# Moving weight-sum transfers, half of a compression and the score matmuls in a decoder-block kernel

## Chip, cores and metric

The kernel runs on one core of one Trainium2 chip. The metric is the device time of one execution in microseconds (us), from runs on the chip, taken as the median of several executions. Beside it there is a hardware profile of one execution, with a record for every instruction of the engines: PE (TensorE, matmuls), PEld (its weight loads), DVE (VectorE), ACT (ScalarE), POOL (GpSimd) and SP (SyncE, which here only issues transfers).

## The reference

One layer of a decoder over 256 positions with 2048 channels, batch 1, float32 throughout:

```
h = rms_norm(x);  p = h @ w_in            # columns: A 2048 | B 2048 | q 1024 | kv 1536 | 48 gates | merge 6144
A: a*sigmoid(g) -> causal depthwise conv (31 taps) -> layer_norm -> silu -> @ w_a_out
B: gelu(uv); u * (tril(W_s) @ layer_norm(v) + b) per chunk of 128, 8 groups -> @ w_b_out
C: 16 heads of 64 in 4 kv groups, three attentions with the same q, summed under sigmoid gates:
     compressed: kc, vc = silu(blocks of 32, stride 16, @ w1) @ w2;  softmax(q kc) vc
     selected:   softmax over 4 blocks of 64 (all 4 are chosen, as top_n = min(16, 4))
     window:     softmax over the last 512 positions (here: all earlier ones)
   -> @ w_c_out
y = (gA*A + gB*B + gC*C) @ w_o;   x = x + rms_norm(y)
u = causal_dwconv3(rms_norm(x) @ w_up)    # 2 x 5632 columns
x = x + rms_norm((silu(u_g) * u_v) @ w_down)
```

## The kernel before

**Number format and main stream.** Every large product is made from operands split into a high part in fp32r (`hi`) and a remainder (`lo`): hi·hi, hi·lo and lo·hi are added up in PSUM. Weights come from HBM in pieces of 128x1024 float32 (512 KB) by `fetch` (L114, issued by SP into five `wraw` buffers in turn). ACT makes `whi` from each (L199), DVE makes `wlo` (L200), and PE multiplies. A piece that feeds the token-major products (`mm_t`, L248 to L251) lasts for twelve matmuls of 512 columns. In order, PE works through: the value half of branch B; the projection columns of A, of u, of the compressed k and v (`wf_c`, first four), of the other k (`wf_c`, last four, tile `kkv`), of v and the head gates, and of q (`wf_q`, tile `qf`); then `branch` (L1148), in which for each of four column blocks `cb` the merge gates of B (`pg`, 96 matmuls) and B's output product (`py<-..Bt`, 48 matmuls) are made; `outs_a` (L1208), A's output product (`py<-..At`, four times 48); the four passes `gates_7` (L1301) for the other merge gates, with C's output product; `w_o`; the feed-forward's up projection (44 rounds, from about 860 us to 1340 us); and `w_down`.

**Seven-product form and the sums of weights.** `gates_7`, `w_o` and `w_down` make some pairs of k-tiles by a form with seven block products in place of eight (class `Seven`, L1041). It needs sums of weight blocks, and these are made by DMA: `ahead_steps` (L134) lists, for 16 + 4 + 33 quads of blocks, copies from HBM to a DRAM tile `ahead` and transfers that add onto it (three to five steps a quad, 204 steps in all). `ahead_by(mark, n)` (L157) puts on POOL's queue a tiny copy `tick<-mark`, which waits until `mark` has been computed, and then the next `n` steps of the list. `pooled` (L124) keeps all of these in one order. The list is thus fixed, and each call only sets when its next part may go out. What is left when the up projection begins is spread over its 44 rounds. The first quads are read back by SP in the first `gates_7` pass (`qa<-ahead`), the last in `w_down`.

**Side work.** Work that belongs to no product of the main stream is written as generators in a queue `bg`. `pump(ns)` (L100) is called after each piece of the main stream and emits steps of `bg` until their stated costs reach `ns` (6500 in `branch` and `outs_a`); `until(name)` emits until a mark is set. Towards the attention the queue holds `cmp_prep(0)` and `cmp_prep(1)` (L681: sums of k or v with the position table, on POOL's memset, DVE and ACT), `cmp_gen(0)` and `cmp_gen(1)` (L701: four 512 KB pieces of `w1` each, 32 matmuls `zp` with 256 columns, then `zs` on ACT, `hp` on PE, tanh, and `kcp` for k or `vcp` for v), and `attn()` (L978). `hold("outputs")` stops the queue until `branch` has come to its block 1. `attn` first runs several generators in turn (`in_turn`, L967, one step of each): `lnz_gen` (L595, the normalised and activated output of A's convolution, tile `At`), `cmp_attn(1)` (L808, the compressed attention of the second 128 positions, ending in `pct`), and the scores of the first attention unit. Then it sets mark `A`, for which `outs_a` waits, and goes through eight units (position half, pair of kv groups, selected or window) with `scores`, `weights` and `values`. The last of them is complete, at the latest, where the first `gates_7` pass calls `attended` (L1315).

**Scores.** q and k are plain float32 and a head has 64 dimensions, so one score matmul uses 64 rows of PE. Two heads lie in the two halves of the partitions (`half`), and `in_turns` (L846) chains their matmuls (r = 1, then 0, for one or two heads of the group at a time, or four) so that they follow each other. Each float32 score matmul shows as two matmul records. The same helper chains the products of probabilities and values (`O`). The PSUM for all side work is a pool of four banks (`bank`, L88).

**What sets the order.** The program is written in Python order, but the order of instructions on each engine is decided by the framework's planner, which simulates the engines and takes the ready instruction of the highest priority; an instruction emitted earlier has the higher priority. `tc.issue_after(ins)` forces an order, and `tc.high_priority(offset=PR)` (PR = 1000) lets an instruction count as if it had been emitted that much earlier. On the chip each engine then works through its own list strictly in order.

Of the kernel before, what the change touches and what calls it, by code (L numbers as in the profile page):

```python
# [64 lines left out]
def block(ctx: ExitStack, tc: tile.TileContext, x, xf, x0, fp, cst, rows, sgw, w1, w2, wf_a, wt_bv, wf_bu, wf_c,  # L65
# [688 lines left out]
        while name not in marks:  # L754
            yield debt[0]

    for kv in range(2):
        bg.append(cmp_prep(kv))
        if kv == 0:
            bg.append(hold("outputs"))  # L760
        bg.append(cmp_gen(kv))

    kkv = s8([128, 2, 1024], F32, "kkv")
    kk = kkv[:, 0].rearrange("p (g b t) -> p g b t", g=2, b=2)
    for i in range(4):
        pc = ftile(wf_c[4 + i], hT)
        fsum(pc, kk[:, i % 2, i // 2], rb=rb)
        ahead_by(kk[:, i % 2, i // 2, 0:1], 1)
        pump(BUDGET)
    vsw = kkv[:, 1].rearrange("p (t c) -> p t c", t=2)  # L770
    gsg = P1.tile([128, 2, 48], F32, name="gsg")
# [22 lines left out]
    for i in range(8):  # L794
        pq = ftile(wf_q[i], hT)
        fsum(pq, qf[:, i], scale=0.125, rb=rb)
        ahead_by(qf[:, i, 0:1], 2 + i % 2)
        pump(BUDGET)


# [2 lines left out]
    def apart(work):  # L803

        for ns in work:
            yield 2.0 * ns
# [39 lines left out]
    def in_turns(work):  # L846


        last = None
        for out, lhsT, rhs, start, stop in work:  # L850
            with ExitStack() as order:
                if last is not None:
                    order.enter_context(tc.issue_after(last))
                last = PE.matmul(out, lhsT=lhsT, rhs=rhs, start=start, stop=stop, skip_group_check=True).ins  # L854

    half = [slice(0, 64), slice(64, 128)]

    class Unit:
# [8 lines left out]
        def scores(self):  # L867
            qt, gg, br = self.at
            nk = (qt + 1) * 128
            mk = cs[:, K_MK + 256 - nk:K_MK + 256]  # L870
            hpb = 512 // nk
            ep = s8([128, 2, 4, 256], F32, f"ep{self.nm}")
            e = self.e = [ep[:, r] for r in range(2)]
            m = self.m = P1.tile([128, 2, 8], F32, tag="am", bufs=2, name="am" + self.nm)
            for b in range(4 // hpb):
                ps = [bank([128, hpb, nk], f"s{self.nm}{b}{r}") for r in range(2)]
                in_turns([(ps[r][:, jj], qf[half[r], gg * 4 + b * hpb + jj, qt * 128:qt * 128 + 128],
                           kk[half[r], gg, br, 0:nk], True, True) for jj in range(hpb) for r in (1, 0)])
                for jj in range(hpb):
                    j = b * hpb + jj  # L880
                    for r in range(2):
                        V.tensor_tensor_reduce(e[r][:, j, 0:nk], ps[r][:, jj], mk, 1.0, -3e38, ALU.add, ALU.max,
                                               m[:, r, j:j + 1])
                        yield nk * 1.05 + 130
            V.tensor_scalar(m[:, :, 0:4], m[:, :, 0:4], -1.0, None, op0=ALU.mult)
# [92 lines left out]
    def attn():  # L978

        units = [Unit(qt, gg, br) for qt in (1, 0) for gg in range(2) for br in range(2)]  # L980
        yield from in_turn(lnz_gen(), apart(cmp_attn(1)), apart(units[0].scores()))
        marks.add("A")
        Ct_box["t"] = s16(P1, [128, 8, 2, T], R, "Ct")
        for n, u in enumerate(units):
            if n + 1 < len(units):
                if n == 1:
                    yield from in_turn(apart(cmp_attn(0)), units[n + 1].scores())
                else:
                    yield from units[n + 1].scores()
            if u.at[2] == 0:  # L990
                V.tensor_mul(spread, pct[u.at[0]][:, u.at[1]][:, None, :].to_broadcast([128, 4, 128]),
                             cs[:, K_RJ:K_RJ + 4][:, :, None].to_broadcast([128, 4, 128]))
            yield from u.weights()
            if SUMS_AT <= n < SUMS_AT + 4:
                yield from input_sums(n - SUMS_AT)
            if u.at[2] == 0:
                O = bank([128, 4, 128], "O" + u.nm)
            yield from u.values(O)
# [149 lines left out]
    def branch():  # L1148

        for cb in range(4):  # L1150
            pg = [PS.tile([128, 512], F32, tag="acc", name=f"pg0{cb}{t}") for t in range(2)]
            for q in range(4):
                hs = granule(wt_g[cb * 4 + q])
                for k in range(4 * q, 4 * q + 4):
                    hi, lo = hs[(k % 4) // 2]
                    c = slice((k % 2) * 512, (k % 2) * 512 + 512)
                    for t in range(2):
                        ts = slice(t * 128, t * 128 + 128)
                        with ExitStack() as order:
                            if (cb, k) == (1, 0):  # L1160
                                order.enter_context(tc.issue_after(norm["v"]))
                            mm_t(pg[t], hT[:, k, 0, ts], hT[:, k, 1, ts], hi[:, c], lo[:, c], k == 0, k == KT - 1)
                if (cb, q) == (0, 2):
                    until("m")
                    debt[0] = 0.0
                elif q < 3:
                    if (cb, q) == (1, 2):
                        marks.add("outputs")
                    pump(BUDGET)
            tgs = {}  # L1170
            for t in range(2):
                for a in range(2):
                    tgs[t, a] = q1(f"mg0{cb}{t}{a}")
                    with tc.high_priority(offset=int(PR)):
                        gated[0] = S.activation(tgs[t, a], pg[t][:, a * 256:a * 256 + 256], AF.Tanh,
                                                scale=rh[:, t:t + 1]).ins
            marks.add("gates")
            pump(BUDGET)
            py = [PS.tile([128, 512], F32, tag="acc", name=f"py0{cb}{t}") for t in range(2)]
            for q in range(2):  # L1180
                hs = granule(wt_p[cb * 2 + q])
                if cb == 0 and q == 0:
                    until("B")
                act = Bt_box["t"]
                for k in range(4 * q, 4 * q + 4):
                    hi, lo = hs[(k % 4) // 2]
                    c = slice((k % 2) * 512, (k % 2) * 512 + 512)
                    for t in range(2):
                        ts = slice(t * 128, t * 128 + 128)
                        with ExitStack() as order:  # L1190
                            if (cb, k) == (0, 7):
                                until("v")
                                debt[0] = max(debt[0], 0.0)
                                order.enter_context(tc.issue_after(norm["v"]))
                            pe_last[0] = mm_t(py[t], act[:, k, 0, ts], act[:, k, 1, ts], hi[:, c], lo[:, c], k == 0, k == 7)
                if q == 0:
                    pump(BUDGET)
            for t in range(2):
                for a in range(2):
                    cc = slice(cb * 512 + a * 256, cb * 512 + a * 256 + 256)  # L1200
                    y = mac[:, t, cc]
                    with tc.high_priority(offset=int(PR)):
                        V.scalar_tensor_tensor(y, tgs[t, a], 1.0, py[t][:, a * 256:a * 256 + 256], op0=ALU.add,
                                               op1=ALU.mult)
            ahead_by(mac[:, 0, cb * 512:cb * 512 + 1], (8, 8, 8, 8)[cb])
            pump(BUDGET)

    def outs_a():  # L1208

        for cb in range(4):  # L1210
            py = [PS.tile([128, 512], F32, tag="acc", name=f"py1{cb}{t}") for t in range(2)]
            for q in range(2):
                hs = granule(wt_p[(4 + cb) * 2 + q])
                if cb == 0 and q == 0:
                    until("A")
                for k in range(4 * q, 4 * q + 4):
                    hi, lo = hs[(k % 4) // 2]
                    c = slice((k % 2) * 512, (k % 2) * 512 + 512)
                    for t in range(2):
                        ts = slice(t * 128, t * 128 + 128)  # L1220
                        pe_last[0] = mm_t(py[t], At[:, k, 0, ts], At[:, k, 1, ts], hi[:, c], lo[:, c], k == 0, k == 7)
                if q == 0:
                    pump(BUDGET)
            for t in range(2):
                with tc.high_priority(offset=int(PR)):
                    V.tensor_copy(ya[:, t, cb * 512:cb * 512 + 512], py[t])
            if cb < 2:
                ahead_by(ya[:, 0, cb * 512:cb * 512 + 1], (8, 4)[cb])
            pump(BUDGET)

    def m_sums(n):
# [772 lines left out]
```

## Time and profile before

| | |
|---|---|
| median of 3 runs | 1563.44 us (1559.46 to 1569.31) |
| time of the profiled execution | 1563.63 us |
| its span, first to last instruction | 1561.9 us |
| busy: PE, DVE, ACT, POOL | 1551.4, 1322.3, 970.2, 220.9 us |
| mean granted TensorE clock | 0.998 |
| HBM read, written | 416.45 MB, 90.44 MB |

All times in the profile are in us from the start of the span, unless marked ns. Consecutive matmuls overlap, and the profile shows for each a duration that includes its way through the array (390 ns for 512 columns). The distance from one start to the next is what a matmul costs in a stream; it is read from the start times in the timeline (16 matmuls of 512 columns in 3.65 us). Where PE waits for less than that overlap, it counts as busy.

### The profile page before, as it was taken

The numbers are of one execution on the slowest core, as the hardware profiler recorded it, in microseconds if no ns is written. First come the engines' busy times: TensorE is split into PE (matmuls) and PEld (weight loads), VectorE is DVE, ScalarE is ACT, GpSimd is POOL, SyncE is SP. The second block draws the span as 40 slices with busy tenths as digits, with TensorE's granted clock in tenths as the row PEclk, the third lists the DMA queues.
The fourth block names the chain that finished last, engine by engine and source line by source line (L and its number), as shares of the span: only waits on it lengthen the run. The fifth ranks groups of instructions, "written<-read, shape, count | busy, mean of one in ns | idle before, by whom it ended". The sixth has DMA issues, their size and how long they took to land.

```text
span 1561.9 us, 23350 instructions
## 1 busy us (share of the span) xinstructions
PE 1551.4 (99%) x8101; PEld 1315.6 (84%) x8101; DVE 1322.3 (85%) x2233; ACT 970.2 (62%) x1536; POOL 220.9 (14%) x349
## 2 busy tenths in 40 slices
PE   9999999999999999999999999999999999999998
PEld 8888889887777778888888888888888888888887
DVE  7899999876766579978886898888888887899898
ACT  7644454455677776656665766566666666577774
POOL 1011351221102100000000032222222221100000
PEclk9999999999999999999999999999999999999999
DMA  9687998999779867777774699999999999989896
GB/s 369 195 268 234 273 300 246 296 303 288 236 215 256 223 230 262 247 227 259 268 256 164 205 301 309 306 335 290 287 280 283 282 284 281 316 287 346 313 375 218
DMA packets 130711, 426.13 MB, mean 273 GB/s; under 512 B 15008, under 2 KB 16784, under 8 KB 129824
## 3 DMA queue, kind: packets, MB, share of 16 engines
q1 hardware_dynamic: 99648, 329.46, 60.2%
q0 software_dynamic: 30368, 94.52, 25.7%
q8 instruction: 63, 1.03, 0.3%
q10 hardware_dynamic: 576, 0.66, 0.1%
q14 instruction: 56, 0.46, 0.1%
HBM read 416.45 MB, written 90.44 MB: 325 GB/s over the span
## 4 chain that ended last, share of the span: by engine, by line
PE 97%; DMA 1%; DVE 1%; ACT 1%; issue 0%; DVEq 0%; ACTq 0%
PE ps L228 29%; PE ps L235 15%; PE pg L1056 8%; PE pd1a L1056 4%; PE pd0b L1056 4%; PE pd0a L1056 3%; PE pd1b L1056 3%; PE py L250 3%; PE py L251 3%; PE py L249 3%; PE poa L1056 2%; PE pg L251 1%; PE pg L250 1%; PE pg L249 1%; PE s L854 1%; PE po L249 1%
## 5 line engine op out<-in xcount | busy, mean ns | idle before, releaser
L200 DVE TENSOR_TENSOR wlo<-wraw,whi 128x1024 fp32r<-128x1024 f32 (+1 forms) x344 | 418.2, 1221 | 92.3 <-ACT whi L199 73.3
L199 ACT ACTIVATE whi<-wraw 128x1024 fp32r<-128x1024 f32 (+1 forms) x344 | 361.8, 1057 | 212.0 <-PE ps L228 117.8
L228 PE MATMUL ps<-h2T,whi 128*128 128x512 f32 x1360 | 317.2, 390 | 0.0
L228 PEld LDWEIGHTS ps<-h2T,whi 128*128 128x128 f32 x1360 | 252.4, 188 | 50.4
L235 PEld LDWEIGHTS ps<-h2T,wlo 128*128 128x128 f32 x1360 | 169.4, 192 | 3.6
L235 PE MATMUL ps<-h2T,wlo 128*128 128x256 f32 x1360 | 170.7, 283 | 0.0
L228 PE MATMUL ps<-hT,whi 128*128 128x512 f32 x640 | 151.9, 390 | 0.0
L228 PEld LDWEIGHTS ps<-hT,whi 128*128 128x128 f32 x640 | 117.9, 188 | 23.0
L1012 DVE TENSOR_TENSOR wlowraw<-wraw,whiwraw 128x1024 fp32r<-128x1024 f32 x74 | 89.7, 1222 | 26.6 <-ACT whiwraw L1012 24.6
L556 DVE SCALAR_TENSOR_TENSOR cv<-hb,fps,cv 128x256 f32<-128x256 f32 x240 | 105.9, 491 | 0.1
L1012 ACT ACTIVATE whiwraw<-wraw 128x1024 fp32r<-128x1024 f32 x74 | 77.9, 1059 | 40.4 <-PE py L251 11.8
L1615 ACT ACTIVATE fa<-fs,fps 128x256 f32<-128x256 f32 x88 | 52.8, 600 | 54.1 <-DVE fs L274 52.3
L235 PEld LDWEIGHTS ps<-hT,wlo 128*128 128x128 f32 x640 | 81.1, 191 | 2.5
L235 PE MATMUL ps<-hT,wlo 128*128 128x256 f32 x640 | 82.8, 283 | 0.0
L1056 PE MATMUL pg<-whiwraw,hT 128*128 128x512 f32 x256 | 82.3, 395 | 0.0
L129 POOL DMA_DIRECT2D ahead<-in_wt_dq_dram x91 | 68.1, 901 | 87.1 <-DMA ahead<-in_wt_dq_dram 87.1
L129 POOL DMA_DIRECT2D ahead<-ahead x53 | 43.5, 822 | 245.4 <-DMA ahead<-in_wt_dq_dram 103.8
L271 ACT ACTIVATE t<-ps 128x256 f32<-128x256 f32 x125 | 47.5, 382 | 49.0 <-PE ps L235 26.3
L129 POOL COPY tick<-gh 128x1 f32<-128x1 f32 x44 | 37.5, 853 | 186.3 <-ACT gh L1623 186.3
L1056 PEld LDWEIGHTS pg<-whiwraw,hT 128*128 128x128 f32 x256 | 47.9, 188 | 10.4 <-issue 0.2
L1616 DVE SCALAR_TENSOR_TENSOR fa<-fs,fps,fa 128x255 f32<-128x255 f32 x88 | 42.4, 481 | 16.6 <-ACT fa L1615 16.5
L272 DVE TENSOR_TENSOR t<-ps,t 128x256 f32<-128x256 f32 x125 | 52.4, 420 | 0.5 <-ACT t L271 0.5
(2520 smaller groups left out, 3317.9 us busy)
## 6 DMA issues: line engine op xcount, KB each, us to landing
wraw<-in_wf_up_dram SPq DMA_DIRECT2D x176, 512.0 KB, 6.6
ahead<-in_wt_dq_dram POOLq DMA_DIRECT2D x74, 512.0 KB, 9.8
wraw<-in_wt_p_dram SPq DMA_DIRECT2D x48, 512.0 KB, 6.4
wraw<-in_wt_dq_dram SPq DMA_DIRECT2D x33, 512.0 KB, 6.0
wraw<-in_wf_a_dram SPq DMA_DIRECT2D x32, 512.0 KB, 5.1
ahead<-in_wt_gq_dram POOLq DMA_DIRECT2D x32, 512.0 KB, 9.9
wraw<-in_wt_g_dram SPq DMA_DIRECT2D x32, 512.0 KB, 7.1
wraw<-in_wt_gp_dram SPq DMA_DIRECT2D x32, 512.0 KB, 4.9
```

The costliest lines, as they stand in the source:

```text
L129: in_pool[:] = [op(*args, **kw).ins]
L199: S.activation(hi[:, :n], raw[:, :n], AF.Copy)
L200: V.tensor_sub(lo[:, :n], raw[:, :n], hi[:, :n].bitcast(F32))
L228: ins = PE.matmul(ps, lhsT=ws[k // 8][0][:, c:c + 128], rhs=mov[:, k], start=bool(k == 0 and first), stop=bool(k == n - 1 and not first), ...
L235: ins = PE.matmul(ps[:, 1], lhsT=ws[k // 8][1][:, c:c + 128], rhs=mov[:, k, 0], start=bool(k == 0 and not first), stop=bool(k == n - 1 and ...
L249: PE.matmul(ps, lhsT=xh, rhs=hi, start=first, stop=False)
L250: PE.matmul(ps, lhsT=xh, rhs=lo, start=False, stop=False)
L251: return PE.matmul(ps, lhsT=xl, rhs=hi, start=False, stop=last).ins
L556: V.scalar_tensor_tensor(ca[:, j], hb[:, j, k:k + T], w(j, k), ca[:, j], op0=ALU.mult, op1=ALU.add)
L1012: seq[eng] = [op(*args, **kw).ins]
L1056: ins = PE.matmul(bank, lhsT=a[x], rhs=w[y], start=first and j == 0, stop=bool(last and j == 2), skip_group_check=more).ins
L1615: S.activation(a, s, AF.Identity, bias=fps[:, C_FB + f:C_FB + f + 1], scale=w[2])
```

## The change

Three things are edited.

1. *Weight-sum transfers.* `ahead_by` is taken out of the four `kkv` tiles (4 steps, and 4 ticks). For q it issues 2 steps a tile where it was 2 and 3 by turns (4 steps fewer). In `branch`, block 0 issues 4 where it was 8 (4 fewer). In `outs_a`, block 1 issues 8 where it was 4, and block 2 issues 4 where there was no call (8 more, one more tick). The remaining 4 come in the up projection, among the rest that is spread there.
2. *Side work.* `cmp_gen(1)`, the second half of the compression, leaves its place in `bg` behind `cmp_prep(1)` and becomes one of the three generators that `attn` runs in turn, with `lnz_gen` and the first unit's scores. `cmp_attn(1)` leaves that group and runs by itself after it, ahead of mark `A`. There its steps count their stated cost once where `apart` made them count twice.
3. *Score runs.* In `in_turns`, every matmul but the first of a chain gets the high priority. In `Unit.scores` the two PSUM banks are requested for r = 1 first and then for r = 0.

```diff
-    for kv in range(2):
-        bg.append(cmp_prep(kv))
-        if kv == 0:
-            bg.append(hold("outputs"))
-        bg.append(cmp_gen(kv))
+    bg.append(cmp_prep(0))
+    bg.append(hold("outputs"))
+    bg.append(cmp_gen(0))
+    bg.append(cmp_prep(1))
...
         fsum(pc, kk[:, i % 2, i // 2], rb=rb)
-        ahead_by(kk[:, i % 2, i // 2, 0:1], 1)
         pump(BUDGET)
...
         fsum(pq, qf[:, i], scale=0.125, rb=rb)
-        ahead_by(qf[:, i, 0:1], 2 + i % 2)
+        ahead_by(qf[:, i, 0:1], 2)
         pump(BUDGET)
...
                 if last is not None:
                     order.enter_context(tc.issue_after(last))
+                    order.enter_context(tc.high_priority(offset=int(PR)))
...
-                ps = [bank([128, hpb, nk], f"s{self.nm}{b}{r}") for r in range(2)]
+                ps = [bank([128, hpb, nk], f"s{self.nm}{b}{r}") for r in (1, 0)][::-1]
...
-        yield from in_turn(lnz_gen(), apart(cmp_attn(1)), apart(units[0].scores()))
+        yield from in_turn(cmp_gen(1), lnz_gen(), apart(units[0].scores()))
+        yield from cmp_attn(1)
         marks.add("A")
...
-            ahead_by(mac[:, 0, cb * 512:cb * 512 + 1], (8, 8, 8, 8)[cb])
+            ahead_by(mac[:, 0, cb * 512:cb * 512 + 1], (4, 8, 8, 8)[cb])
...
-            if cb < 2:
-                ahead_by(ya[:, 0, cb * 512:cb * 512 + 1], (8, 4)[cb])
+            if cb < 3:
+                ahead_by(ya[:, 0, cb * 512:cb * 512 + 1], (8, 8, 4)[cb])
```

## The prediction

> **What bounds the kernel.** I read the page first, for who is busy and what the chain that ended last is made of.
>
> ```profile
> span 1561.9 us, 23350 instructions
> ...
> PE 1551.4 (99%) x8101; PEld 1315.6 (84%) x8101; DVE 1322.3 (85%) x2233; ACT 970.2 (62%) x1536; POOL 220.9 (14%) x349
> ...
> q0 software_dynamic: 30368, 94.52, 25.7%
> ...
> PE 97%; DMA 1%; DVE 1%; ACT 1%; issue 0%; DVEq 0%; ACTq 0%
> ```
>
> PE is the bound: 99% busy and 97% of the chain. No product is removed by the change, so only two things can shorten it: time in which PE waits or runs at a lower clock, and pairs of matmuls that could run at once and don't. The second hides in "busy", so I look for it in start times. The first I look for by stage, with the view that gives busy times for stretches (columns: PE, PEld, DVE, ACT and POOL busy, granted clock, DMA share, GB/s).
>
> ```profile
> 335.00:360.00 25.00, 24.88 (x122) 20.75 (x120) 20.17 (x32) 12.53 (x16) 6.09 (x16) 1.00 1.02 307
> 360.00:380.00 20.00, 17.69 (x94) 14.53 (x95) 14.67 (x23) 15.29 (x23) 2.10 (x5) 1.00 0.87 312
> 380.00:400.00 20.00, 18.65 (x82) 15.19 (x82) 11.18 (x15) 8.40 (x12) 3.63 (x6) 0.91 0.99 296
> 430.00:500.00 70.00, 70.00 (x344) 53.76 (x343) 48.72 (x120) 50.45 (x118) 9.95 (x17) 1.00 0.83 232
> 500.00:548.00 48.00, 48.00 (x258) 33.63 (x256) 26.06 (x96) 37.68 (x110) 7.29 (x11) 1.00 0.85 229
> 548.00:570.00 22.00, 20.89 (x94) 14.48 (x93) 11.59 (x18) 16.23 (x39) 0.00 (x0) 1.00 0.65 209
> 880.00:1340.00 460.00, 460.00 (x2645) 407.16 (x2644) 396.08 (x693) 286.53 (x458) 104.26 (x154) 1.00 0.95 287
> 395.47:398.88 3.41, 3.41 (x9) 2.63 (x8) 3.27 (x8) 3.14 (x5) 0.06 (x1) 0.50 1.09 320
> ```
>
> PE is idle for 0.12 + 2.31 + 1.35 = 3.8 us between 335 and 400, with the DMA engines full (shares of 1.02, 0.87 and 0.99), and for 1.1 us between 548 and 570. Behind the last of the first group 3.41 us pass at a clock of 0.50, worth 1.7 us. In the up projection (880 to 1340) nothing is lost, though the DMA share is 0.95. Who released these waits, from the view of waits between 340 and 400, and then the chain of that stretch (start, length):
>
> ```profile
> PE hp L720 <- ACT zs L716: 1.3, 1, 1.3
> PE py L249 <- ACT whi L199: 1.3, 2, 0.7
> PE py L250 <- DVE wlo L200: 0.6, 1, 0.6
> PE pg L250 <- DVE wlo L200: 0.5, 1, 0.5
> ```
>
> ```profile
> 352.94 9.74 DMA wraw<-in_wt_p_dram
> ...
> 380.87 11.16 DMA wraw<-in_wt_g_dram
> ...
> 393.19 0.28 ACT zs L716
> 393.51 1.16 PE hp L720 x8
> ```
>
> All four have one cause. Weight pieces land late, ACT's `whi` is held, and what stands behind it in ACT's order (`zs` at 393.19) or depends on it (`wlo`) is late for PE. Two transfers make the chain here, of 9.7 and 11.2 us. How late that is, from the page's and this stretch's (335 to 400) DMA issues, median us to landing last:
>
> ```profile
> wraw<-in_wt_p_dram SPq DMA_DIRECT2D x48, 512.0 KB, 6.4
> wraw<-in_wt_p_dram SPq DMA_DIRECT2D x8, 512.0 KB, 10.9
> ```
>
> So 3.7 us of waits and 1.7 us of half clock, 5.4 us, is what this stage can give back.
>
> **Part 1, the transfers.** Their number and their engine time, from the view of line 129:
>
> ```profile
> L129 POOL DMA_DIRECT2D ahead<-in_wt_dq_dram x91: 544/830/2217, 442.4 to 1331.7; - x91
> L129 POOL DMA_DIRECT2D ahead<-ahead x53: 801/814/874, 92.6 to 1341.5; - x53
> L129 POOL DMA_DIRECT2D ahead<-in_wt_gq_dram x48: 533/816/897, 72.9 to 352.4; - x48
> L129 POOL DMA_DIRECT2D ahead<-in_wt_oq_dram x12: 627/822/1133, 352.9 to 441.8; - x12
> ```
>
> These are 204 steps, and the software queue that carries them took 25.7% of 1561.9 us = 401 us of all sixteen engines: 2.0 us a step at most, some of it being other transfers. Four steps fewer at block 0 take 8 us out of the 25 us from 335 on, a share of 0.70 where 1.02 is. The eight taken from `kkv` and q would have gone out before, where PE loses nothing; they let POOL, which works strictly in order, reach block 0's and 1's calls, and the memsets of the compression that stand behind them, without arrears. POOL also loses four ticks and gains one, at no cost: nothing on the path waits for POOL but these transfers and memsets.
>
> Where do they go? Eight go behind `outs_a`'s blocks 1 and 2, from about 500 us on: 16 us of DMA. Free there are 0.15 x 48 + 0.35 x 22 = 14.9 us by the rows above. That is just enough, if they spread. If they don't, the first seven-form pass, which fetches on SP in the same stretch, meets what 335 to 400 met: at worst the same 5.4 us. At best it costs nothing, as from 880 to 1340, where a share of 0.95 costs PE nothing. I take 1.0, near the lower end, because the share at 430 to 548 leaves room and PE has no wait there now. Four steps in the up projection add 8 us to 460, a share of 0.97: nothing, and if that cover failed, the pieces there would land later for a few rounds. No sum becomes late: the steps for the gate passes are out by block 2 of `branch` (64 steps in the list's order), and the last pass that reads them comes after `outs_a`, three passes on.
>
> **Part 2, the moved half.** `cmp_gen(1)` issues four fetches of `w1` and one of `w2` on SP, four `whi` and `wlo`, two `zs`, 32 matmuls `zp`, then `hp` and `vcp`. All of this remains, at the same price on PE; it only moves, in turn with `lnz_gen` and the scores, so its four pieces, 2 MB beside the main stream, come spread out. The main stream's fetches no longer stand behind four extra ones in the five buffers. `lnz_gen` comes forward and is needed only by `outs_a`; a block of `branch` lies between. `cmp_attn(1)` starts later; `O` of the first unit waits for its `pct`, and behind that `O` on PE's order stands the main stream. The first two kinds of wait in the list (1.3 + 0.6 + 0.5 = 2.4 us, for `whi` and `wlo`) I count as gone, since both the transfers and the pieces that crowd them leave. The wait for `zs` with the half clock (1.3 + 1.7 = 3.0 us) goes from here, but the same `hp` behind the same `zs` behind a `whi` comes again somewhere after 400: I count half, 1.5 us, between 0 and 3.0. Together 3.9 us.
>
> The row of the clock says that it fell within 2 us of a wait of 1.3 us. [...]
>
> **Part 3, the runs of scores.** From the timeline of PE (start, length; the next row's start is the end of the run): a cut run and a whole one with 256 columns, then a whole and a cut one with 128.
>
> ```profile
> 404.81 0.70 PE L854 MATMUL s<-kkv,qf 64*128 64x256 f32 x2
> 405.43 0.50 PE L251 MATMUL pg<-whi,hT 128*128 128x512 f32 x1
> ...
> 407.47 1.13 PE L854 MATMUL s<-kkv,qf 64*128 64x256 f32 x6
> 408.52 0.50 PE L250 MATMUL pg<-wlo,hT 128*128 128x512 f32 x1
> ...
> 452.40 1.13 PE L854 MATMUL s<-kkv,qf 64*128 64x256 f32 x8
> 453.46 0.50 PE L250 MATMUL pg<-wlo,hT 128*128 128x512 f32 x1
> ...
> 531.61 1.16 PE L854 MATMUL s<-kkv,qf 64*128 64x128 f32 x16
> 532.71 0.50 PE L250 MATMUL py<-wlo,At 128*128 128x512 f32 x1
> ...
> 542.42 0.49 PE L854 MATMUL s<-kkv,qf 64*128 64x128 f32 x2
> 542.83 0.50 PE L1056 MATMUL pg<-whiwraw,hT 128*128 128x512 f32 x1
> ...
> 544.43 1.16 PE L854 MATMUL s<-kkv,qf 64*128 64x128 f32 x14
> 545.51 0.50 PE L1056 MATMUL pg<-whiwraw,hT 128*128 128x512 f32 x1
> ```
>
> Whole, a run of eight records takes 1.06 us; cut behind its first matmul, 0.62 + 1.05 = 1.67 us. [...] With 128 columns it is 1.10 against 0.41 + 1.08 = 1.49. Four of the eight long runs and three of the four short ones are cut, the first and the last of them shown: 4 x 0.61 + 3 x 0.39 = 3.6 us. Priority for everything behind the first matmul is what would close them; the bound below is zero, and less if a chained `O` moves ahead of main work while its probabilities are still being copied (one such wait is worth 1.3 us, like `zs`). A run also needs its second bank, from four that transposes and `O` share; five of twelve whole today show that both are often free. I take 2.5 us.
>
> **Sum.** 2.5 + 3.9 - 1.0 = 5.4 us off the profiled execution's 1563.63 us, 1558.2; the median shown is 0.2 us lower, so 1558.
>
> **The rivals.** *Nothing changes* (0.22): the planner already put `hp` and the products where the chip was late for them, so other waits of the same sum arise when it lays them out anew, and runs stay cut for want of a bank. 1563. For it: the waits in the list are all places where PE's fixed order met late data, and the change moves data, not the rule.
>
> *Slower, by the attention's end* (0.12). The wait at 548 to 570 is
>
> ```profile
> PE pg0s L1056 <- DVE Ct L933: 1.1, 1, 1.1
> ```
>
> The first seven-form pass needs the bank of the last `O`, which `Ct` frees. The moved half puts four `whi` into ACT's attention stretch:
>
> ```profile
> L199 ACT ACTIVATE whi<-wraw 128x1024 fp32r<-128x1024 f32 x31 | 32.4, 1061 | 29.2 <-PE pg L251 12.7 <-DMA wraw<-in_wt_p_dram 6.4 <-DMA wraw<-in_wt_g_dram 3.7
> ```
>
> If `Ct` comes later by 4 x 1.06 = 4.2 us, and the longer wait halves the clock as at 395 (1.7), that is 5.9 us; with the scores' 2.5 won and the other waits merely displaced, 1563.4 + 5.9 - 2.5 = 1567. It decides once `Ct` is over 2.5 us later. Against it: 50.45 of 70 and 37.68 of 48 us of ACT leave room, and the side work's stated cost ahead of the units is no larger.
>
> *All of it* (0.13): every cut, every wait and the 1.1 us at `Ct`, 3.6 + 5.4 + 1.1 = 10.1 us: 1553.
>
> *The clock stretch stays* (0.08), whatever PE waits for: half of 1.7 is lost from the sum, 1559. [...]
>
> **The numbers.** The forecast has 0.45: 1558. The range of 8 in 10 runs from *all of it* to the *slower* case, half of each left out, 1553 to 1567. About 1% (15.6 us) is what a measurement of this kernel can tell from no change. Faster than that would need half as much again as all that I found (10.1 us), 0.02; slower, almost three times the slower rival, or a fault of order that I don't see, 0.03; within, 0.95.
>
> **What would show it.** Right: no PE wait for `whi` or `wlo` between 335 and 400, a DMA share there well under 1, pieces of `wt_p` landing in some 7 us; score rows of x8 and x16 only; the clock at 1.00 throughout; the wait at `pg0s` no longer than 1.1. Wrong: x2 rows among the scores, PE waits after 400 for `zs`, `pt` or a bank, a share over 1 between 500 and 570 with waits in the first gate pass, or a new stretch at 0.50.

## The result and the profile after

The changed kernel took 1554.61 us (median of 6, 1553.81 to 1556.28), beside 1564.67 us for the kernel before on the same chip (median of 6, 1559.46 to 1571.14). The ratio is 0.993, 95% interval 0.9909 to 0.9952: about 10 us less. Forecast were 1558 and a gain of 5.4 us. The profiled executions went from 1563.63 to 1554.34 us, 9.3 us less.

The page of the changed kernel: PE's idle time is nearly gone.

```profile
span 1552.6 us, 23345 instructions
...
PE 1546.2 (100%) x8101; PEld 1313.3 (85%) x8101; DVE 1322.1 (85%) x2233; ACT 968.7 (62%) x1536; POOL 220.6 (14%) x346
```

Its stretches (columns: PE, PEld, DVE, ACT and POOL busy, granted clock, DMA share, GB/s), then everything PE waited for in the whole execution:

```profile
335.00:360.00 25.00, 25.00 (x126) 21.29 (x125) 21.43 (x32) 16.02 (x22) 3.19 (x11) 1.00 0.90 268
360.00:380.00 20.00, 20.00 (x107) 16.80 (x107) 17.11 (x36) 16.08 (x29) 3.05 (x6) 1.00 0.77 231
380.00:400.00 20.00, 19.57 (x104) 16.20 (x103) 14.58 (x33) 14.04 (x31) 2.70 (x4) 1.00 1.03 336
430.00:500.00 70.00, 70.00 (x342) 50.91 (x342) 48.17 (x135) 49.39 (x122) 10.45 (x18) 1.00 0.76 212
500.00:548.00 48.00, 48.00 (x255) 34.73 (x253) 26.30 (x81) 37.33 (x106) 10.70 (x18) 1.00 0.94 260
548.00:570.00 22.00, 22.00 (x97) 17.27 (x96) 16.94 (x18) 14.03 (x17) 0.60 (x2) 1.00 0.92 296
880.00:1340.00 460.00, 460.00 (x2630) 406.52 (x2629) 394.48 (x688) 282.74 (x449) 107.00 (x162) 1.00 0.98 296
```

```profile
PE warm L343 <- DVE wz L340: 1.1, 1, 1.1
PE hp L720 <- ACT zs L716: 0.4, 1, 0.4
```

From 335 to 400 PE is idle for 0.43 us where it was 3.8, and the clock stays at 1.00. From 548 to 570 it is idle for nothing where it was 1.1, although the DMA share there rose from 0.65 to 0.92. The first wait is the start of the program. So the idle time and the half clock that went are 3.35 + 1.7 + 1.1 = 6.2 us of the 9.3. What did not come is in the timeline of PE (start, length): of the cut score runs two with 256 columns (a third begins at 418.27) and one with 128 (the other at 506.51).

```profile
435.54 0.70 PE L853 MATMUL s<-kkv,qf 64*128 64x256 f32 x2
438.07 1.13 PE L853 MATMUL s<-kkv,qf 64*128 64x256 f32 x6
...
471.03 0.70 PE L853 MATMUL s<-kkv,qf 64*128 64x256 f32 x2
477.77 1.13 PE L853 MATMUL s<-kkv,qf 64*128 64x256 f32 x6
...
486.28 0.48 PE L853 MATMUL s<-kkv,qf 64*128 64x128 f32 x2
491.91 0.49 PE L853 MATMUL s<-kkv,qf 64*128 64x128 f32 x4
```

Three long and two short runs are cut, where it was four and three: one of each fewer, 1.0 us by the prediction's prices. That makes 7.2 of 9.3 us. The other 2 us are not assigned by these rows; waits shorter than the overlap of matmuls (one of 512 columns shows 0.39 us where the next starts after 0.23) count as busy and are not seen in them.

### The profile page after: what moved, and what is told of

It reads as the page before. It is cut to its first block, busy times and chain, and to the rows that moved or that the text cites. A ratio compares the mean times of both kernels' runs of the same rounds, so it can differ in the third digit from the quotient of the medians.

```text
span 1552.6 us, 23345 instructions
## 1 busy us (share of the span) xinstructions
PE 1546.2 (100%) x8101; PEld 1313.3 (85%) x8101; DVE 1322.1 (85%) x2233; ACT 968.7 (62%) x1536; POOL 220.6 (14%) x346
## 4 chain that ended last, share of the span: by engine, by line
PE 97%; DVE 1%; DMA 1%; ACT 0%; issue 0%; DVEq 0%; ACTq 0%
PE ps L228 29%; PE ps L235 15%; PE pg L1056 8%; PE pd1a L1056 4%; PE pd0b L1056 3%; PE pd1b L1056 3%; PE py L249 3%; PE py L250 3%; PE py L251 3%; PE pd0a L1056 2%; PE poa L1056 2%; PE pg L250 2%; PE pg L251 2%; PE pg L249 2%; PE po L249 1%; PE po L251 1%
## 5 line engine op out<-in xcount | busy, mean ns | idle before, releaser
L129 POOL DMA_DIRECT2D ahead<-in_wt_dq_dram x91 | 71.6, 918 | 84.1 <-DMA ahead<-in_wt_dq_dram 65.0
```

The source lines that it names most:

```text
L129: in_pool[:] = [op(*args, **kw).ins]
```

## The experiments

Each is compared with the kernel before on its own chip. `only1`, `only2`, `only3` and `p12` share one (before there: 1564.57 us, 27 runs, 1560.04 to 1568.71); `only_b`, `only_kqo`, `both1` and `both` another (1564.9, 29 runs, 1560.64 to 1570.95); `only_t`, `after_nob`, `after2` and `both2` a third (1562.0, 21 runs, 1559.4 to 1567.01). `after2` is the changed kernel once more; on the third chip the change is worth 7.0 us by the medians (ratio 0.9949, 0.9935 to 0.9963), not 10.

### Each part alone, and parts 1 and 2 together

`only1` has the edits of `ahead_by` alone.

```diff
-        ahead_by(kk[:, i % 2, i // 2, 0:1], 1)
-        ahead_by(qf[:, i, 0:1], 2 + i % 2)
+        ahead_by(qf[:, i, 0:1], 2)
-            ahead_by(mac[...], (8, 8, 8, 8)[cb])
+            ahead_by(mac[...], (4, 8, 8, 8)[cb])
-            if cb < 2:
-                ahead_by(ya[...], (8, 4)[cb])
+            if cb < 3:
+                ahead_by(ya[...], (8, 8, 4)[cb])
```

> Only the transfers are moved (the 12 steps, as in the change); side work and score runs as before. The lists of PE, DVE, ACT and SP are those of before; only POOL's differs. Theory T (the waits between 335 and 400 come from the moved transfers crowding the weight pieces): those waits and the half clock go, 5 to 6 us less than before, about 1559; the wait at the attention's end (1.1 us) stays. Theory L (the new lists of the engines no longer put work where data is late): nothing goes, 1564.

Measured: 1557.04 us (10 runs, 1555.95 to 1558.56), ratio 0.9956 (0.9941 to 0.9971), 7.5 us less. In the traces of the two kernels only POOL's list of instructions differs. Two of its stretches, and PE's waits (that at the start of the program left out):

```profile
335.00:360.00 25.00, 25.00 (x123) 21.20 (x122) 22.59 (x35) 16.02 (x19) 3.55 (x12) 1.00 0.91 263
...
380.00:400.00 20.00, 19.82 (x105) 16.56 (x105) 9.78 (x14) 9.34 (x16) 2.69 (x4) 1.00 1.03 328
```

```profile
PE pg0s L1055 <- DVE Ct L932: 1.1, 1, 1.1
PE pv L479 <- ACT swraw L170: 0.4, 1, 0.4
PE hp L720 <- ACT zs L716: 0.2, 1, 0.2
```

Although the moved half of the compression is still in its old place, the waits for `whi` and `wlo` are gone. No half clock is seen either, but one trace can't show that it was removed: `only3`, below, is without it too. The wait for `Ct` stays.

`only2` moves `cmp_gen(1)` and `cmp_attn(1)` alone.

```diff
-    for kv in range(2):
-        bg.append(cmp_prep(kv))
-        if kv == 0:
-            bg.append(hold("outputs"))
-        bg.append(cmp_gen(kv))
+    bg.append(cmp_prep(0))
+    bg.append(hold("outputs"))
+    bg.append(cmp_gen(0))
+    bg.append(cmp_prep(1))
...
-        yield from in_turn(lnz_gen(), apart(cmp_attn(1)), apart(units[0].scores()))
+        yield from in_turn(cmp_gen(1), lnz_gen(), apart(units[0].scores()))
+        yield from cmp_attn(1)
```

> Only the second half of the compression is moved into attn and cmp_attn(1) behind it; transfers and score runs as before, POOL's list is that of before. T: the crowded stage stays crowded, waits of 2.4 us or more for whi and wlo remain between 335 and 400; only the attention's end is gained, 2 to 3 us, about 1562. L: waits and half clock go and the attention ends earlier, about 1555.

Measured: 1561.25 us (12 runs, 1559.17 to 1568.16), ratio 0.9989 (0.9973 to 1.0004): 3.3 us between the medians, not told from zero by itself. Its two largest waits of PE, and the stretch with the second of them:

```profile
PE py L249 <- ACT whi L199: 2.5, 2, 1.3
PE hp L720 <- ACT zs L716: 1.3, 1, 1.3
```

```profile
390.00:400.00 10.00, 8.73 (x45) 6.83 (x44) 5.98 (x9) 6.77 (x12) 2.69 (x4) 1.00 1.04 351
```

The stalls of this stage stay; the wait for `Ct` is no longer in the list. The moved half frees the end of attention and does not relieve the crowded stage.

`only3` has the priority and the order of bank requests alone.

```diff
                     order.enter_context(tc.issue_after(last))
+                    order.enter_context(tc.high_priority(offset=int(PR)))
-                ps = [bank(...) for r in range(2)]
+                ps = [bank(...) for r in (1, 0)][::-1]
```

> Only the priority inside the score runs and the order of the two bank requests. Compared as lists, every engine's instructions stand in the same order as before, so both theories expect no change, 1564 to 1565, and score rows cut as before (x2 and x6 where a run of x8 is cut). The forecast of 2.5 us for this part would show as 1562.

Measured: 1564.9 us (12 runs, 1560.73 to 1570.46), ratio 1.0003 (0.9986 to 1.002). No change that can be told. The reason stands in the trace: the lists of PE, DVE, ACT, POOL and SP are those of the kernel before, operation by operation and tile by tile. So this is also a second profiled execution of the same lists. It took 1561.36 us where the first took 1563.63, and it has neither the wait for `zs` nor the half clock of that one:

```profile
380.00:400.00 20.00, 19.41 (x92) 16.02 (x93) 12.23 (x17) 8.74 (x13) 4.33 (x7) 1.00 1.00 301
```

The waits for `whi` (1.5 us) and `wlo` (1.4) are there again.

`p12` has the edits of `only1` and `only2` without those of `only3`.

> Transfers and moved half, without the third part. Lists in the same order as those of the whole change. Both theories: the time of the whole change, 1554.6 (within 0.1%), so the third part is worth nothing; if the third part had a share, 1557.

Measured: 1554.12 us (6 runs, 1553.5 to 1555.3), ratio 0.9939 (0.992 to 0.9958): the whole change. Its lists are those of the changed kernel, on every engine. So -7.5 for the transfers, -3.3 for the moved half and nothing for the runs of scores stand against -10.4 for the first two together; the intervals don't tell the sum from that.

### Which of the transfers

`only_b` issues four steps fewer at block 0 of `branch`; `only_kqo` makes the other eight moves.

```diff
-            ahead_by(mac[...], (8, 8, 8, 8)[cb])     # only_b
+            ahead_by(mac[...], (4, 8, 8, 8)[cb])
```

> Four transfer steps fewer at the first block of branch, nothing else (they go out in the up projection instead). All three transfer edits together gave -7.5 us. Theory 'the block's own count' (what crowds 335 to 400 is what is issued there): these four give most of it, -5 to -7 us, median 1558 to 1559.5, no wait of PE for whi or wlo between 335 and 400. Rival 'arrears' (POOL reaches the block late because of the steps at k and q, so the count at the block matters little): -2 us or less, waits for whi and wlo of 1 to 3 us remain, DMA share 335 to 360 stays near 1.0.

> The other eight steps alone: none at k, two at each q, eight and four behind the second and third block of outs_a; the first block of branch keeps eight. Theory 'the block's own count': -2 us or less, waits for whi and wlo remain. Rival 'arrears': -5 us or more, and POOL's last tick on qf comes near 312 instead of 327. If the two parts add up, this and the four steps together make -7.5.

`only_b` took 1559.8 us (12 runs, 1557.03 to 1566.1), ratio 0.997 (0.9954 to 0.9986). `only_kqo` took 1560.45 us (12 runs, 1559.22 to 1562.02), ratio 0.9979 (0.9969 to 0.999). Both theories hold in part and neither alone: -5.1 and -4.4 us. In both kernels only POOL's list differs from before. Together the twelve steps give 7.5 by the medians, less than the sum of 9.5, so some of what each part saves may be the same loss; the intervals (2.2 to 7.2, 1.6 to 4.9 and 4.5 to 9.2 us) are too wide to show it. POOL's last tick on `qf` comes at 311.5 us in `only_kqo`, as *arrears* foresaw, and at 331.9 in `only_b`. The two differ in width: `only_kqo` spreads over 2.8 us, `only_b` over 9. The waits say why. First `only_b` (waits of PE, then of ACT, then POOL's timeline):

```profile
PE pg L249 <- ACT whi L199: 1.1, 1, 1.1
...
PE pg L250 <- DVE wlo L200: 0.8, 1, 0.8
```

```profile
ACT bk L694 <- POOL bt L687: 8.8, 1, 8.8
```

```profile
347.22 0.55 POOL L687 MEMSET bt<- 128x16 f32 x4
```

then `only_kqo` (waits of PE, a line of its DMA issues from 335 to 400, and POOL's timeline):

```profile
PE py L249 <- ACT whi L199: 1.4, 2, 1.0
...
PE pg L250 <- DVE wlo L200: 0.6, 1, 0.6
```

```profile
wraw<-in_wt_p_dram SPq DMA_DIRECT2D x8, 512.0 KB, 10.0
```

```profile
338.19 0.86 POOL L687 MEMSET bt<- 128x16 f32 x4
```

In `only_b` pieces land early (7.8 us is its median for this row), but ACT stands 8.8 us before `bk` in `cmp_prep(1)`, because POOL reaches the memset `bt` only at 347.2, behind the steps of q and the first block; a `whi` that is behind `bk` on ACT is then late for PE. There an `ahead` step of the first block stands for 8.53 us until an earlier transfer has landed; in the profiled execution before the same step stood for 3.89 us. In `only_kqo` POOL is there at 338.2 and ACT does not wait for it; the pieces still land after 10.0 us and PE waits for those. Two causes, then: the landing time, which the four steps weigh on most, and POOL's arrears, which the eight early steps set. The prediction's "All four have one cause" is not borne out.

`after_nob` is the changed kernel with the first block's count back at 8.

```diff
-            ahead_by(mac[...], (4, 8, 8, 8)[cb])
+            ahead_by(mac[...], (8, 8, 8, 8)[cb])
```

> The changed kernel with one thing undone: the first block of branch issues eight steps again (four fewer then go out in the up projection). Taken alone these four steps gave -5.1 us. Theory 'crowding' (the waits come from what is issued there, wherever the half of the compression runs): +2 to +4 us over the changed kernel and a wider spread, waits for whi or wlo between 335 and 400. Rival 'either is enough' (with the half moved away or the early steps gone the rest fits): less than +1 us, no wait there.

Measured: 1559.19 us (10 runs, 1556.86 to 1562.09), against 1554.98 for the changed kernel beside it (`after2`, below): ratio of the means 1.0026 (1.0019 to 1.0033), 4.2 us by the medians, and a spread of 5.2 us where `after2` has 2.0. Its waits (that at the start left out) and its DMA row:

```profile
PE py L249 <- ACT whi L199: 1.1, 2, 0.7
PE hp L720 <- ACT zs L716: 0.8, 1, 0.8
```

```profile
wraw<-in_wt_p_dram SPq DMA_DIRECT2D x8, 512.0 KB, 9.8
```

Crowding is confirmed where everything else is as in the change; *either is enough* falls. POOL is not behind here: it comes to the memset `bt` at 337.1, and ACT doesn't wait for it. In the changed kernel this row is

```profile
wraw<-in_wt_p_dram SPq DMA_DIRECT2D x8, 512.0 KB, 8.6
```

and `after2`, on the same chip as `after_nob`, has 9.2 there with no wait of PE. So between these two kernels 0.6 us of this median separates pieces that come in time from pieces that PE waits for.

### Whole runs of scores

`both1` is the kernel before with both banks of each run taken by DVE before PE can start; `both` is `p12` with the same two lines.

```diff
                 ps = [bank([128, hpb, nk], f"s{self.nm}{b}{r}") for r in range(2)]
+                V.memset(ps[0][:, 0, 0:1], 0.0)
+                V.tensor_copy(ps[1][:, 0, 0:1], ps[0][:, 0, 0:1])
```

> The kernel before, with two small DVE instructions ahead of each run of scores: a memset of one column in the first of the run's two banks, and a copy of that column into the second bank, so that both banks are taken before the first matmul can start. 24 DVE instructions more, the result is the same. Theory 'second bank': the cut runs of the kernel before were cut because the second bank was still taken; now PE's order has only whole runs, and by the prices of the profile before (4 x 0.61 + 3 x 0.39) the time falls by 2.5 to 3.6 us, median 1561 to 1562. Rival 'the cover is gone': banks held empty make transposes and O late, PE waits for pt, pp or O; 0 to +3 us. Rival 'the price was wrong' (a cut run hides its cost beside the neighbours): whole runs, no waits, and no change of the time.

Measured: 1560.5 us (12 runs, 1555.95 to 1567.12), ratio 0.9974 (0.9958 to 0.999). All twelve runs are whole on the chip; the first and the last:

```profile
415.37 1.14 PE L854 MATMUL s<-kkv,qf 64*128 64x256 f32 x8
...
549.15 1.16 PE L854 MATMUL s<-kkv,qf 64*128 64x128 f32 x16
```

That is what the theory of the second bank foresaw, though that the two instructions also put off the start of a run can't be told apart from it here. PE waits for no `pt`, `pp` or `O`, so *the cover is gone* falls. The time is less, and the interval (1.6 to 6.6 us) holds the 2.5 to 3.6 foreseen; but the two instructions also change the order of other work on PE, DVE and ACT, so the whole of it can't be put down to the cuts. Its profiled execution took 1567.12 us and shows POOL's arrears at their worst (PE's wait, ACT's wait, POOL's timeline):

```profile
PE pg L249 <- ACT whi L199: 7.2, 1, 7.2
```

```profile
ACT bk L694 <- POOL bt L687: 14.9, 1, 14.9
```

```profile
338.51 1.92 POOL L129 DMA_DIRECT2D ahead<-in_wt_gq_dram  x3
340.11 0.69 POOL L129 COPY tick<-mac 128x1 f32<-128x1 f32 x1
350.17 0.82 POOL L129 DMA_DIRECT2D ahead<-ahead  x1 [9.38 <-DMA ahead<-in_wt_gq_dram]
...
352.72 0.55 POOL L687 MEMSET bt<- 128x16 f32 x4
```

An `ahead` step stands for 9.38 us until an earlier transfer has landed, and the memset behind it on POOL takes ACT and then PE with it. The granted clock falls as well, to 0.50 from 352.87 to 359.69. The two kernels of the case show the same place in these two rows, before and after (timeline of POOL):

```profile
342.46 0.56 POOL L687 MEMSET bt<- 128x16 f32 x4
```

```profile
336.95 0.86 POOL L687 MEMSET bt<- 128x16 f32 x4
```

This place goes with the eight early steps: in the six profiled kernels that issue them at k and q (before, `only2`, `only3`, `only_b`, `both1`, `only_t`) the memset comes between 341.2 and 352.7 us, in the eight others between 336.9 and 338.2. In the profiled execution before, ACT waited 3.9 us for this memset, and PE was idle for only 0.12 us from 335 to 360; whether the later waits go back to it in part is not shown.

> Parts one and two of the change (1554.1 us, without priority and bank order) with the same two small DVE instructions ahead of each run of scores. In PE's order all long runs are whole, two short ones are cut after the third of their eight matmuls. Theory 'second bank': three cuts of long runs fewer, -1.8 us, median 1552.0 to 1552.7, which would be faster than the change. Rival 'cover gone': 1554 to 1557, with PE waits for pt, pp or O. Rival 'price wrong': 1554, no new waits.

Measured: 1554.23 us (6 runs, 1552.14 to 1555.24), ratio 0.9937 (0.992 to 0.9954): no difference from `p12` that can be told across two chips. It was run again beside the changed kernel.

> The changed kernel once more, to stand on the same chip as the next. Both theories: 1553.8 to 1555.5.

> Parts one and two of the change with both score banks taken ahead of each run, once more, beside the changed kernel on the same chip. Theory 'the price holds' (three cut long runs fewer at 0.61 us, as in this kernel's first trace): -1.2 to -1.8 us against the changed kernel, ratio of the two medians 0.9990. Rival 'given back' (the banks held empty cost as much elsewhere): within 0.3 us of the changed kernel.

Measured: `after2` 1554.98 us (6 runs, 1554.22 to 1556.19), `both2` 1553.43 us (6 runs, 1552.84 to 1554.42). The ratio of the means is 0.9990 (0.9986 to 0.9994), 1.55 us less (0.9 to 2.2): the price holds within that interval, *given back* falls, and this version beats both kernels. In its timeline the runs that the change left cut are whole at 256 columns:

```profile
439.22 1.13 PE L852 MATMUL s<-kkv,qf 64*128 64x256 f32 x8
...
478.49 1.13 PE L852 MATMUL s<-kkv,qf 64*128 64x256 f32 x8
...
491.35 0.71 PE L852 MATMUL s<-kkv,qf 64*128 64x128 f32 x6
493.00 0.93 PE L852 MATMUL s<-kkv,qf 64*128 64x128 f32 x10
```

Three cuts for 1.55 us are 0.52 us each, if all of it is theirs; the prediction had 0.61. By the start times the first short run gives 0.2 us of it: it is in two pieces where the changed kernel has it in three (x2, x4 and x10 from 486.28 on). Two short runs are still cut, one behind its third matmul and one, from 507.05 on, behind its fifth, with both banks taken and products for `O` between the pieces; why, stays open.

### The end of attention

`only_t` moves `cmp_attn(1)` alone.

```diff
-        yield from in_turn(lnz_gen(), apart(cmp_attn(1)), apart(units[0].scores()))
+        yield from in_turn(lnz_gen(), apart(units[0].scores()))
+        yield from cmp_attn(1)
```

> Of the moved half only the place of cmp_attn(1): its stated cost is no longer counted beside the first scores, but behind them, as in the change; cmp_gen(1) stays where it was. Theory 'stated cost' (the units of attention end earlier because cmp_attn(1) is no longer worked off in turn): the wait for Ct at pg0s (1.1 us) goes, the other waits stay, -1 to -2 us. Rival 'the half itself' (the end of attention is freed because cmp_gen(1) takes part of the pump's time away from the main stream ahead of it): the wait of 1.1 us at pg0s stays, time as before.

Measured: 1560.68 us (12 runs, 1559.95 to 1566.19), ratio 0.9994 (0.9982 to 1.0006): by time not told from nothing. In its stretches the wait is gone, and its DMA share shows that the transfers are where they were:

```profile
335.00:360.00 25.00, 25.00 (x124) 21.17 (x123) 20.84 (x34) 13.04 (x16) 6.07 (x16) 1.00 1.01 310
...
548.00:570.00 22.00, 22.00 (x99) 16.41 (x99) 14.50 (x16) 12.64 (x15) 0.00 (x0) 1.00 0.59 188
```

So it is the place and stated cost of `cmp_attn(1)` that free `Ct`; `cmp_gen(1)` need not move for it. The wait of 1.1 us stands in all six profiled kernels that keep the old place and in none of the eight with the new one. What it is worth in time is not shown: 1.1 us is smaller than the interval, and the profiled execution has a wait of the same size in `w_o` that the one before has not:

```profile
PE po L249 <- ACT h2k L199: 1.1, 1, 1.1
```

Four long and three short score runs are cut in this kernel, as before. The one of each kind that `only2` and the changed kernel close comes with the move of `cmp_gen(1)`.

## Why the prediction was right or wrong

The place was right: PE's waits between 335 and 400 with the half clock behind them, and the wait at `pg0s`. The time lies in the range, but nearly at *all of it* (1553), and the three terms of the sum were each mis-sized or put to the wrong part. That it lies inside is in part luck: against the parts measured alone, the sum is 8.5 us short for part 1, 0.6 too high for part 2 and 2.5 too high for part 3, and the last two take back some of the first.

**Part 1, the transfers (forecast: a cost of 1.0 us; measured alone: 7.5 us less).** The step that failed is that its gain was priced at nothing by itself and its relief was counted under part 2. `only1` removes the waits with the half compression still in place; `only_b`, `only_kqo` and `after_nob` confirm it. The size of the relief was off too: four steps fewer were to take 8 us out of the DMA engines and bring the share from 335 to 360 to 0.70, and pieces were to land in some 7 us. Measured are a share of 0.90 (0.91 in `only1`) and 8.6 us; over 335 to 400 the shares add up to 58.5 us of DMA time where they were 62.7, 4.2 us less. PE's waits went all the same. The cost of 1.0 us for the eight steps behind `outs_a` was not seen: the share is 0.94 and 0.92 there and PE is idle for nothing. The cover named for the up projection held at 0.98, where 0.97 was worked out.

POOL's arrears were named in the text, ahead of the memsets, and left without a price; they cost PE 7.2 us in the one execution of `both1` that was profiled. This may be why the stage returns more than the 5.4 us counted there: that number was read from one execution of a kernel that spreads over 8 to 12 us, while `only1` and the changed kernel spread over 2 to 3. The profiled one is about 1 us from the median of its chip, though, so a mild execution alone doesn't explain it. That the longest executions before hold such waits for POOL was not seen directly; it is inferred from `both1` and from `only_kqo`, which narrows the spread to 2.8 us where `only_b` keeps 9.

**Part 2, the moved half (forecast 3.9; measured alone 3.3, interval -0.6 to 4.2).** The size is within the interval and the reason fails. The waits for `whi` and `wlo` stayed in `only2` (2.5 us) and the `zs` wait too (1.3). What it gave is the wait for `Ct`, which the sum had left out and only *all of it* counted, and one whole score run of each kind, from the new order. The expectation that `hp` behind `zs` would come again after 400 was wrong in place, and half right in kind: it is at 389, and PE waits 0.4 us for it.

**Part 3, the runs (forecast 2.5; measured 0).** The step that failed is "priority for everything behind the first matmul is what would close them". It closes nothing: no engine's order changes. The sentence behind it, that a run needs its second bank, is what the runs bear out: with both banks taken first, all twelve runs of the kernel before are whole. The price agrees within the noise, 0.52 us for 0.61. In the prediction's own rows the six records behind a cut take 1.05 us and a whole run of eight 1.06, so the first two, 0.62 us by themselves, save nothing in the rest. The sign that was named for failure, x2 rows among the scores, is there after the change.

**The rivals.** *Nothing changes* and *slower, by the attention's end* fell: four more `whi` in ACT's stretch did not delay `Ct`. *All of it* is nearest in time, but not in its parts: 6.2 us of idle time and clock, 1.0 of its 3.6 us of cuts, and 2 us that no row assigns.

**The clock stretch.** It is in none of the profiles with all edits of part 1, but `only2`, `only3` and `only_t` are without it as well, so the profiles alone don't settle *the clock stretch stays*. The mean granted clock of every execution does better. It is 0.998 or less, as in the profiled execution before, in 15 of 77 executions of the kernel before and in 30 of 137 of all kernels that keep the eight early steps, and in none of 62 of the others (`only1`, `only_kqo`, `after_nob`, `p12`, `both`, `both2` and both sets of the changed kernel). The rival falls for losses of that size. A mean of 0.999 can still hide one stretch, as it does in the profiled `only_b`. No run shows a stretch that comes whatever PE waits for: the three seen begin 1.96 us (the kernel before) and 1.28 us (`only_b`) behind a wait of PE, and 4.9 us into one (`both1`).

## What to carry to other kernels

Where a helper engine works strictly in order, count what stands behind each of its long waits, and follow it: here a memset behind a DMA step on POOL (which stood for 9.38 us in `both1`) held an activation on ACT (14.9 us), that held a weight split, and PE paid (7.2 us). A priority can reorder only what is ready; where a pair of matmuls needs two buffers, take both before the first may start (`both1`: twelve whole runs, where five were). Price a stage's stalls from several executions if the kernel's times spread: two profiles of the same lists, before and `only3`, differ by the wait for `zs` and 1.7 us of half clock.

## What the hardware showed that was not expected

Half clock goes with waits of PE, but not with each of them. Between 335 and 400 us it lasts 3.41 us in the kernel before (395.47 to 398.88) and in `only_b` (352.24 to 355.65), and 6.82 us in `both1` (352.87 to 359.69); the eleven other profiles show 1.00 there. In the kernel before a wait of 1.35 us ends 1.96 us ahead of the fall. The rows are first from `only_b`, the time ahead of the fall with most of two waits of PE, 1.10 and 0.76 us, and the stretch itself; then from `only2`; then from `both1`, where a wait of 7.23 us begins at 347.97:

```profile
348.83:352.24 3.41, 1.79 (x7) 1.25 (x8) 2.95 (x6) 3.41 (x5) 0.26 (x2) 1.00 0.93 189
352.24:355.65 3.41, 3.41 (x12) 2.83 (x11) 3.41 (x10) 1.22 (x2) 0.13 (x1) 0.50 0.92 214
```

```profile
360.00:370.00 10.00, 7.45 (x34) 5.33 (x32) 3.68 (x4) 7.01 (x10) 0.00 (x0) 1.00 1.02 356
```

```profile
346.04:349.45 3.41, 1.93 (x9) 1.27 (x7) 0.00 (x0) 0.00 (x0) 0.00 (x0) 1.00 0.87 316
349.45:352.87 3.42, 0.00 (x0) 0.00 (x0) 0.00 (x0) 0.00 (x0) 2.56 (x8) 1.00 0.28 29
```

In the kernel before the eight matmuls of 512 columns that start in the stretch are 0.43 us apart, and 0.23 us behind it: 1.6 us more, where 3.41 us at 0.50 were counted as 1.7. In the 3.41 us ahead of the fall PE was idle for 1.35 us in the kernel before, for 1.62 in `only_b` and all the time in `both1`. In `only2` 2.55 us of idle time from 360 to 370 and 1.27 us from 390 to 400 left the clock at 1.00, and in `both1` the clock stayed at 1.00 for 3.42 us behind the first 1.48 us of the wait. So by these rows idle time alone doesn't decide, and what does, no run here shows.
